# A hybrid mixer layer on one core: the rwkv chain's next state copied by ScalarE, the decayed state's share of kappa put into the next PSUM bank, and work that waits for transfers issued later

## The chip, the core and the metric

The kernel runs on one core of a Trainium2 chip. The core has TensorE (PE, matrix multiply, with its weight loads shown as PEld), VectorE (DVE), ScalarE (ACT), GpSimd (POOL) and SyncE (SP, which issues the transfers here). Each engine takes its own list of instructions in order, and semaphores hold an instruction until what it needs is done. The metric is the time of one execution on the device, in microseconds (us); lower is better.

## The reference

One layer over a sequence of 1024 frames and 1024 channels, all in float32: RMS norm, one input projection, three mixers side by side (4 heads mLSTM, 6 heads retention, 6 heads RWKV-7), output projection with residual, RMS norm, a gated feed-forward with residual, and a last RMS norm.

```python
h = rmsnorm(x, ln1_g);  p = h @ w_in
pm, pr, pw = jnp.split(p, [M_COLS, M_COLS + R_COLS], axis=-1)
y = jnp.concatenate([mlstm_group(pm, ...), retention_group(pr), rwkv7_group(pw, ...)], axis=-1)
x = x + y @ w_out
h = rmsnorm(x, ln2_g)
x = x + (jax.nn.silu(h @ w_gate) * (h @ w_up)) @ w_down
return rmsnorm(x, lnf_g)
# the recurrence inside rwkv7_group, one frame:
S = (S * w_t[:, :, None, :]
     - jnp.einsum('bhvk,bhk->bhv', S, kk_t)[..., None] * (kk_t * a_t)[:, :, None, :]
     + v_t[..., :, None] * k_t[..., None, :])
y_t = jnp.einsum('bhvk,bhk->bhv', S, r_t)
```

## The kernel before

The projections and the feed-forward split each float32 operand into a high and a low part and multiply in three matmuls (`three`, `tok_proj`, `product`); these are the bulk of PE's work. The program has two parts. In the first, up to about 767 us, the mixers run, woven into the bulk matmuls of the input and output projections. The second part is the feed-forward.

In the first part each piece of work is a Python generator. `weave` runs them against a planned clock: each `yield (cost, wait)` says how much PE time the step takes and how long until its next step is due, and names ("inv00", "yw3") are events that others wait for. The chain's wait after a chunk is `CHAIN`, after its inner steps `LAT`. Generators in `sharing` (rwkv_proj, fillers, out_proj) fill the time between. The framework's scheduler then puts each engine's instructions into one fixed list, by its own estimate of when each is ready; an instruction that waits holds up everything behind it on its engine.

RWKV works on 3 pairs of heads (i), each in two halves of 512 frames (h), each half in 8 chunks of 64 frames (c): 48 chunks in a row. For each half,

- `rwkv_half` prepares the operands: the decayed keys and queries in the big tile E, the gram matmuls between `kb` and E (L460; q is the head of the pair, and the two heads lie in the two halves of the partitions), their masks on DVE, and the transposed keys;
- `rwkv_inverse` inverts the triangular 64 x 64 blocks: the blocks go through DRAM (`ab_d`) into MN, one 32 x 32 block in each partition; ACT copies parts of MN into R (L509); 15 elimination steps on DVE work on R and MN; R goes back through DRAM (`r_d`) into E; a transpose (L535) and small matmuls (L540, L546) join the blocks;
- `rwkv_chain_pair` walks the chunks. Per chunk: kappa = E . X (L581), where X holds the state and the values of the chunk; ACT copies it to pm (L583); pm times the inverse (L586) gives the corrected values, which ACT copies into X (L592, L593); then the state's part of the output (L590), the new state (L597) and the output (L600). DVE adds the decayed old state and writes the sum into the next chunk's X (L607), POOL copies it to st (L609); ACT copies the output to yw (L610) and sums its squares (L611).

`rwkv_out` fetches the gate and the bonus and multiplies them on POOL (L638) before it waits for yw. `mlstm_load` fetches the log gates of a chunk as w, adds the causal mask on POOL (L860) and takes the exponential on ACT (L863). `norms` splits the stored output (ywt) into high and low. The rotary table `rot` is loaded once, 512 KB. PSUM has eight banks in three pools: acc (3), misc (3) and chain (2).

Of the kernel before, what the change touches and what calls it, by code (L numbers as in the profile page):

```python
# [19 lines left out]
P = 128  # L20
# [3 lines left out]
KT = 8  # L24
# [30 lines left out]
def trunk_kernel(ctx: ExitStack, tc: tile.TileContext, a: dict, out: bass.AP):  # L55
# [71 lines left out]

    def signal(name, after=0.0):
        events[name] = clock[0] + after
# [61 lines left out]
    CHAIN, INV, ATT, NORM, MIX = 3.51, 20.16, 3.09, 3.26, 1.28  # L191
# [178 lines left out]

    hv, hv_E = {}, {}
# [9 lines left out]
    def rwkv_half(i, h, r, k, v):  # L381
# [64 lines left out]
        E = big.tile([P, 8, 2, 256], F32, name="E", tag="E")  # L446
        kb = sb.tile([P, 8, 2, 64], F32, name="kb", tag="kb")
        for q in range(2):
            rows = rows_of(q)
            V.tensor_tensor(kb[rows, :, q, :], c3(th)[rows], c3(ek)[rows], ALU.mult)  # L450
            V.tensor_tensor(kb[rows, :, 1 - q, :], c3(k)[rows], c3(ek)[rows], ALU.mult)
            V.tensor_tensor(E[rows, :, q, 128:192], c3(kk)[rows], er[rows, :, 0:64], ALU.mult)
            G.tensor_tensor(E[rows, :, q, 192:256], c3(r)[rows], er[rows, :, 1:65], ALU.mult)
        yield 0.9, 5.5
        for c0 in range(0, 8, 4):
            grams = [misc_tile().rearrange("p (c x) -> p c x", c=4) for _ in two]
            for c in range(4):
                for q, g4 in enumerate(grams):
                    rows = rows_of(q)
                    PE.matmul(g4[:, c, :], lhsT=kb[rows, c0 + c, :, :].rearrange("p a t -> p (a t)"),  # L460
                              rhs=E[rows, c0 + c, q, 128:256], start=True, stop=True)
            for q, g4 in enumerate(grams):
# [3 lines left out]
                V.tensor_tensor(E[orow, cs4, q, 192:256], g4[rows, :, 0:64], msk[rows], ALU.mult)  # L466
                V.tensor_tensor(E[orow, cs4, q, 128:192], g4[orow, :, 0:64], msk[orow], ALU.mult)
                V.tensor_tensor(E[:, cs4, q, 64:128], g4[:, :, 64:128],
# [8 lines left out]
        for c0 in range(0, 8, 4):  # L477
# [4 lines left out]
            S.copy(out=E[:, c0:c0 + 4, :, 0:64], in_=pt.rearrange("p (c q d) -> p c q d", c=4, q=2))  # L482
# [7 lines left out]
    col = lambda b: slice(192 + b * 32, 224 + b * 32)  # L490
    lane = lambda g: slice(32 * g, 32 * g + 32)

    def rwkv_inverse_issue(i, h, E):
        ab_d = dram.tile([2, 2, 8, 32, 32], F32, name="ab_d", tag=f"ab_d{i}{h}")
        for q in range(2):
            for b in range(2):
                SY.dma_start(out=ab_d[b, q].rearrange("c s t -> s c t"), in_=E[blk(q, b), :, q, col(b)])
        return ab_d

    def rwkv_inverse():  # L500
        for i in range(3):
            for h in range(2):
# [5 lines left out]
                for g in range(4):  # L508
                    S.copy(out=R[lane(g)], in_=MN[lane(g), g::4, :])  # L509
# [4 lines left out]
                V.tensor_tensor(tv, mf[:, 34:34 + 15 * 66:66].unsqueeze(2).broadcast_to([P, 15, 32]), MN[:, 2:31:2], ALU.mult)  # L514
# [15 lines left out]
                for q in range(2):  # L530
                    for b in range(2):
                        SY.dma_start(out=E[blk(q, b), :, q, col(b)], in_=r_d[b, q].rearrange("c s t -> s c t"))
                yield 0.0, 7.5
                for q in range(2):
                    V.transpose(out=T11[blk(q, 0)], in_=E[blk(q, 0), :, q, col(0)])  # L535
                pqr = misc_tile()
                q3, r3 = (pqr[:, z:z + 256].rearrange("p (c t) -> p c t", c=8) for z in (0, 256))
                for c in range(8):
                    for q in range(2):
                        PE.matmul(q3[blk(q, 1), c, :], lhsT=E[blk(q, 0), c, q, col(1)], rhs=T11[blk(q, 0), c, :],  # L540
# [3 lines left out]
                for c in range(8):  # L544
                    for q in range(2):
                        PE.matmul(r3[blk(q, 0), c, :], lhsT=Q[blk(q, 1), c, :], rhs=E[blk(q, 1), c, q, col(1)],  # L546
                                  start=True, stop=True)
                for q in range(2):
                    S.copy(out=E[blk(q, 0), :, q, col(1)], in_=r3[blk(q, 0)])
# [7 lines left out]
    def rwkv_chain_pair(i):  # L557
        st = None
        for h in range(2):
# [3 lines left out]
            for c in range(8):  # L563
# [14 lines left out]
                chn = chain_tile()  # L578
                pm = sb.tile([P, 64], F32, name="pm", tag="pm", bufs=2)
                for q in range(2):  # L580
                    PE.matmul(chn[rows_of(1 - q), 0:64], lhsT=E[:, c, q, 128:192], rhs=X[:, c, q, :],  # L581
                              start=True, stop=True, skip_group_check=True)
                S.copy(out=pm, in_=chn[:, 0:64])  # L583
                yield 0.2, LAT
                for q in range(2):
                    PE.matmul(chn[rows_of(q), 64:128], lhsT=E[rows_of(1 - q), c, q, 192:256], rhs=pm[rows_of(1 - q), :],  # L586
                              start=False, stop=True, skip_group_check=True)
                for q in range(2):
                    d, o = rows_of(q), rows_of(1 - q)
                    PE.matmul(chn[o, 192:256], lhsT=E[d, c, q, 192:256], rhs=st[d, :], start=False, stop=False,  # L590
# [972 lines left out]
```

## Time and profile before

| | us |
|---|---|
| median of 3 runs (1514.54 to 1521.72) | 1515.08 |
| the profiled execution | 1521.67 |
| its span in the profile | 1519.9 |
| PE busy in it | 1425.6 |
| DVE, ACT, POOL busy | 892.4, 556.2, 437.9 |

The page of the profile gives the busy time of each engine, the chain of work that ended last, and groups of instructions by line; waits name the engine's instruction, what it waited for, the total, the times and the longest. Names such as `E<-misc` are output and input tiles of the program. The granted clock (PEclk) is the share of full speed that PE's throttle let through. Busy PE includes the modelled ends of matmuls that overlap.

### The profile page before, as it was taken

The page shows a single profiled execution, that of the slowest core. Times are in us where ns is not written, and L with a number is a line of the kernel's source. Part 1 is how long each engine was busy: PE and PEld are TensorE (multiplying, and loading weights), DVE is VectorE, ACT ScalarE, POOL GpSimd, SP SyncE. Part 2 cuts the span into 40 slices and gives each one's busy share as a digit, 9 for nine tenths or more (in the row PEclk, how much of TensorE's full clock was granted, in tenths as well). Part 3 has the DMA queues.
Part 4 walks back from the last instruction along what each step waited for, and adds up shares of the span by engine and source line. Part 5 has one row for each costly group of instructions (what it writes and reads, how often), then busy time and mean ns, then how long its engine had stood idle before and what let it go on. Part 6 is the DMA issues. An engine that isn't in the chain of part 4 may idle for free.

```text
span 1519.9 us, 23085 instructions
## 1 busy us (share of the span) xinstructions
PE 1425.6 (94%) x8434; PEld 1161.3 (76%) x8434; DVE 892.4 (59%) x1762; ACT 556.2 (37%) x1202; POOL 437.9 (29%) x539
## 2 busy tenths in 40 slices
PE   7998799789998998999998999999999998999996
PEld 5777577777777887887777887888888886887886
DVE  6457567458847756645468555555555565347434
ACT  6353334333432133244456333333333344224222
POOL 3211013234424333333545433344444420000000
PEclk9999999999978889899999999999999999999998
DMA  5142122334422244354632222222222247337333
GB/s 209 43 136 66 50 80 74 83 89 112 122 59 68 85 129 124 106 161 142 220 112 85 96 83 83 72 73 78 83 84 83 83 168 255 93 95 238 98 97 111
DMA packets 122269, 164.55 MB, mean 108 GB/s; under 512 B 38028, under 2 KB 70956, under 8 KB 120876
## 3 DMA queue, kind: packets, MB, share of 16 engines
q1 hardware_dynamic: 122156, 163.08, 33.5%
q8 instruction: 66, 1.08, 0.3%
q14 instruction: 47, 0.39, 0.1%
HBM read 124.75 MB, written 38.29 MB: 107 GB/s over the span
## 4 chain that ended last, share of the span: by engine, by line
PE 53%; DVE 3%; POOL 2%; DMA 2%; issue 1%; ACT 0%; POOLq 0%; DVEq 0%; SPq 0%; ACTq 0%
PE acc L1171 5%; PE acc L1172 5%; PE acc L1173 5%; PE chain L1365 5%; PE chain L1364 5%; PE chain L1366 5%; PE misc L1172 4%; PE misc L1171 4%; PE misc L1173 4%; PE acc L119 2%; PE acc L121 2%; PE acc L120 2%; DVE act L93 1%; PE acc L729 1%; PE acc L731 1%
## 5 line engine op out<-in xcount | busy, mean ns | idle before, releaser
L93 DVE TENSOR_TENSOR wlo<-wraw,whi 128x512 fp32r<-128x512 f32 (+1 forms) x210 | 147.9, 707 | 138.3 <-ACT whi L90 137.1
L90 ACT ACTIVATE whi<-wraw 128x512 fp32r<-128x512 f32 (+1 forms) x210 | 128.1, 612 | 226.3 <-PE chain L1365 117.9
L729 PE MATMUL acc<-whi,act 128*128 128x256 f32 (+1 forms) x512 | 161.3, 318 | 4.4 <-ACT whi L90 3.4
L90 ACT ACTIVATE whi<-rg 128x512 fp32r<-128x512 f32 x128 | 79.8, 631 | 228.7 <-POOL rg L1232 90.0
L730 PE MATMUL acc<-wlo,act 128*128 128x256 f32 (+1 forms) x512 | 155.4, 305 | 5.2 <-DVE wlo L93 5.2
L119 PE MATMUL acc<-act,whi 128*128 128x512 f32 x352 | 152.3, 433 | 7.0 <-ACT whi L90 6.2
L93 DVE TENSOR_TENSOR wlo<-rg,whi 128x512 fp32r<-128x512 f32 x128 | 93.1, 728 | 108.1 <-ACT whi L90 105.9
L731 PE MATMUL acc<-whi,act 128*128 128x256 f32 (+1 forms) x512 | 153.0, 300 | 0.0
L1364 PE MATMUL chain<-act,whi 128*128 128x512 f32 (+1 forms) x374 | 144.3, 386 | 4.0 <-ACT act L90 4.0
L120 PE MATMUL acc<-act,whi 128*128 128x512 f32 x352 | 145.5, 413 | 1.5 <-DVE act L252 1.5
L121 PE MATMUL acc<-act,wlo 128*128 128x512 f32 x352 | 145.7, 414 | 1.1 <-DVE wlo L93 1.1
L1365 PE MATMUL chain<-act,whi 128*128 128x512 f32 (+1 forms) x374 | 144.0, 385 | 0.5 <-DVE act L93 0.5
L1366 PE MATMUL chain<-act,wlo 128*128 128x512 f32 (+1 forms) x374 | 143.8, 384 | 0.0
L1171 PE MATMUL acc<-act,whi 128*128 128x512 f32 x352 | 139.3, 396 | 3.4 <-ACT pre L1432 2.7
L1173 PE MATMUL acc<-act,wlo 128*128 128x512 f32 x352 | 138.8, 394 | 0.0
L1172 PE MATMUL acc<-act,whi 128*128 128x512 f32 x352 | 138.5, 394 | 0.0
L729 PEld LDWEIGHTS acc<-whi,act 128*128 128x128 f32 x512 | 104.3, 205 | 12.1 <-ACT whi L90 3.9
L730 PEld LDWEIGHTS acc<-wlo,act 128*128 128x128 f32 x512 | 105.0, 206 | 9.2 <-DVE wlo L93 6.7
L731 PEld LDWEIGHTS acc<-whi,act 128*128 128x128 f32 x512 | 105.2, 206 | 1.0
L1172 PE MATMUL misc<-act,whi 128*128 128x512 f32 x264 | 104.1, 394 | 0.0
L1171 PE MATMUL misc<-act,whi 128*128 128x512 f32 x264 | 104.0, 394 | 0.0
L1173 PE MATMUL misc<-act,wlo 128*128 128x512 f32 x264 | 103.8, 393 | 0.0
(327 smaller groups left out, 2835.9 us busy)
## 6 DMA issues: line engine op xcount, KB each, us to landing
wraw<-in_w_down SPq DMA_DIRECT2D x85, 256.0 KB, 2.7
rg<-in_w_gate SPq DMA_DIRECT2D x22, 512.0 KB, 4.9
rg<-in_w_up SPq DMA_DIRECT2D x22, 512.0 KB, 5.0
a_dram<-work SPq DMA_DIRECT2D x41, 256.0 KB, 2.2
wraw<-in_w_tm SPq DMA_DIRECT2D x40, 256.0 KB, 3.0
rg<-a_dram SPq DMA_DIRECT2D x10, 1024.0 KB, 6.1
v_dram<-vt SPq DMA_DIRECT2D x64, 128.0 KB, 1.9
wraw<-in_w_out SPq DMA_DIRECT2D x32, 256.0 KB, 3.2
```

The lines of the kernel that those rows point to most:

```text
L90: S.activation(hi, src, AF.Copy, scale=scale)
L93: (eng or V).tensor_tensor(lo, src, hi.bitcast(F32), ALU.subtract)
L119: PE.matmul(ps, lhsT=hi, rhs=xh[:, k, :], start=(k == 0), stop=False)
L729: PE.matmul(o, lhsT=xh[h][:, k, sl], rhs=w[k][0], start=(k == 0), stop=False)
L730: PE.matmul(o, lhsT=xh[h][:, k, sl], rhs=w[k][1], start=False, stop=False)
L731: PE.matmul(o, lhsT=xl[h][:, k, sl], rhs=w[k][0], start=False, stop=(k == KT - 1))
L1171: PE.matmul(ps, lhsT=hi, rhs=hi_x[:, k, :], start=(start and k == 0), stop=False, skip_group_check=True)
L1172: PE.matmul(ps, lhsT=hi, rhs=lo_x[:, k, :], start=False, stop=False, skip_group_check=True)
L1173: PE.matmul(ps, lhsT=lo, rhs=hi_x[:, k, :], start=False, stop=(stop and k == 3), skip_group_check=True)
L1364: PE.matmul(ps, lhsT=hi, rhs=hi_a[:, sl], start=(f == 0), stop=False)
L1365: PE.matmul(ps, lhsT=hi, rhs=lo_a[:, sl], start=False, stop=False)
L1366: PE.matmul(ps, lhsT=lo, rhs=hi_a[:, sl], start=False, stop=(f == FT - 1))
```

## The change

The chunk's algebra is regrouped. X for the next chunk now holds only the new part of the state, which two ACT copies move there from the bank. The decayed old state, sd, is made on POOL at the start of the chunk; its product with the next chunk's kappa columns goes into the next chunk's bank (`nxt`) ahead, and the next chunk's kappa adds onto it (`start=first`). DVE writes only st. E is laid out so that one matmul with 128 output rows gives new state and output ("both"); the output of a head then lies beside the state of the other, and yw and Square work on half the partitions each. Beside that:

- R is loaded from `ab_d` by a transfer of its own; the four ACT copies go.
- The gram matmuls are held in the order in which the heads alternate, each issued after the one before (`tc.issue_after`).
- `late(eng)` issues what follows after the last instruction written so far on that engine. It is used for the first step of the inverse and the transposes (DVE), the product of gate and bonus (POOL), the split of ywt (ACT), and the mLSTM mask and exponential, which move out of the load into `mlstm_weights`.
- rot is loaded per frame tile, 64 KB, 24 times through two buffers.
- CHAIN is 1.4 instead of 3.51, and the planned costs of the steps are 0.4, 0.2, 0.6 instead of 0.2, 0.2, 0.4.

```diff
+    def late(eng):
+        return tc.issue_after(next(i for i in reversed(nc.cur_bb.bb.instructions) if i.engine == eng.engine))
-    CHAIN, INV, ATT, NORM, MIX = 3.51, 20.16, 3.09, 3.26, 1.28
+    CHAIN, INV, ATT, NORM, MIX = 1.4, 20.16, 3.09, 3.26, 1.28
+    kap = lambda q: slice(256 + 128 * q, 320 + 128 * q)
+    rcp = lambda q: slice(320 + 128 * q, 384 + 128 * q)
...
-                    PE.matmul(g4[:, c, :], lhsT=kb[rows, c0 + c, :, :].rearrange("p a t -> p (a t)"),
-                              rhs=E[rows, c0 + c, q, 128:256], start=True, stop=True)
+                    with tc.issue_after(prev.ins) if prev else nullcontext():
+                        prev = PE.matmul(g4[:, c, :], lhsT=kb[rows, c0 + c, :, :].rearrange("p a t -> p (a t)"),
+                                         rhs=E[rows, c0 + c, 256 + 128 * q:384 + 128 * q], start=True, stop=True)
...
-                for g in range(4):
-                    S.copy(out=R[lane(g)], in_=MN[lane(g), g::4, :])
+                SY.dma_start(out=R, in_=ab_d.rearrange("b q c (j g) t -> g (b q c) j t", g=4))
...
-                V.tensor_tensor(tv, mf[:, 34:34 + 15 * 66:66].unsqueeze(2).broadcast_to([P, 15, 32]), MN[:, 2:31:2], ALU.mult)
+                with late(V):
+                    V.tensor_tensor(tv, mf[:, 34:34 + 15 * 66:66].unsqueeze(2).broadcast_to([P, 15, 32]), MN[:, 2:31:2], ALU.mult)
...
-                chn = chain_tile()
+                chn = chain_tile() if first else nxt
+                both = lambda q: slice(128 + 64 * q, 192 + 64 * q)
...
+                if not last:
+                    nX, nE, n = (X, E, c + 1) if c < 7 else (hv[i, 1]["X"], hv[i, 1]["E"], 0)
+                    sd = sb.tile([P, 64], F32, name="sd", tag="sd", bufs=2)
+                    G.tensor_scalar(sd, st, dl[:, c:c + 1], None, ALU.mult)
...
+                if not last:
+                    nxt = chain_tile()
+                    for q in range(2):
+                        d, o = rows_of(q), rows_of(1 - q)
+                        PE.matmul(nxt[o, 0:64], lhsT=nE[d, n, kap(q)], rhs=sd[d, :], start=True, stop=False,
+                                  skip_group_check=True)
...
+                        PE.matmul(chn[:, both(q)], lhsT=E[:, c, 128 * q:128 * q + 128], rhs=X[:, c, q, :], start=False,
+                                  stop=True, skip_group_check=True)
...
-                        V.scalar_tensor_tensor(nX[d, n, q, :], in0=st[d, :], scalar=dl[d, c:c + 1],
-                                               in1=chn[d, 128:192], op0=ALU.mult, op1=ALU.add)
-                        G.tensor_copy(nst[d, :], nX[d, n, q, :])
-                S.copy(out=yw[:, c % 4, :], in_=chn[:, 192:256])
+                        S.copy(out=nX[d, n, q, :], in_=chn[d, both(q)])
+                    for q in range(2):
+                        d = rows_of(q)
+                        V.scalar_tensor_tensor(nst[d, :], in0=st[d, :], scalar=dl[d, c:c + 1], in1=chn[d, both(q)],
+                                               op0=ALU.mult, op1=ALU.add)
+                for q in range(2):
+                    o = rows_of(1 - q)
+                    S.copy(out=yw[o, c % 4, :], in_=chn[o, both(q)])
+                    S.activation(sb.tile([P, 64], F32, name="ysq", tag="ysq")[o, :], chn[o, both(q)], AF.Square,
+                                 accum_out=var[o, c % 4:c % 4 + 1])
...
+                    with late(G):
+                        G.tensor_tensor(add, add, ga, ALU.mult)
...
+            if g in (2, 3, 4):
+                rot = at.tile([P, P], F32, name="rot", tag="rot", bufs=2)
+                SY.dma_start(out=rot, in_=a["rot"][:, t, :])
...
+    def mlstm_weights(c, ws):
+        for q, w in enumerate(ws):
+            G.tensor_tensor(w, w, cc("causal").unsqueeze(1).broadcast_to([P, 2, P]), ALU.add)
+            for p in range(2):
+                hd = 2 * p + q
+                S.activation(w[:, p, :], w[:, p, :], AF.Exp, scale=-1.0, bias=mg["gs"][:, c, hd:hd + 1])
...
+                with late(S):
+                    split_hi(yh[:, 5 + i], yw)
```

The edits change every engine's list. Three places show how; line numbers of the changed kernel differ. First ACT before, in the chain of the third pair's first half, where the inverse of its second half begins:

```order
L583 COPY pm<-chain 128x64
L509 COPY R<-MN 32x256 x4
L755 ACTIVATE vt<-acc,rhalf 128x256
L592 COPY X<-chain 64x64
L593 COPY X<-chain 64x64
L90 ACTIVATE whi<-wraw 128x512 x3
```

ACT after, where the preparation of the same half ends (L491 is the copy of its transposed keys; L597 is now pm, L606 and L607 the corrected values, L631 the next X, L638 yw, L639 the squares):

```order
L491 COPY E<-misc 128x4x2x64 x2
L639 ACTIVATE ysq,yvar<-chain 64x64
L638 COPY yw<-chain 64x64
L639 ACTIVATE ysq,yvar<-chain 64x64
L597 COPY pm<-chain 128x64
L606 COPY X<-chain 64x64
L607 COPY X<-chain 64x64
L631 COPY X<-chain 64x64 x2
```

The copies of R between pm and X are gone; the next X follows the corrected values, and yw of the chunk before stands ahead of pm here.

Second PE before, one chunk of the first pair's second half (L586 to L600; L729 to L731 are bulk matmuls of a token projection):

```order
L586 MATMUL chain<-pm,E 64x64 x2
L590 MATMUL chain<-st,E 64x64 x2
L729 MATMUL acc<-whi,act 128x256 x2
L730 MATMUL acc<-wlo,act 128x256
L731 MATMUL acc<-whi,act 128x256
L597 MATMUL chain<-X,E 64x64 x2
L600 MATMUL chain<-X,E 64x64 x2
```

PE after, the end of an early chunk (L611 is the state's part of the output, L617 the decayed state's kappa for the next chunk, L625 "both"; L119 to L121 are bulk matmuls):

```order
L611 MATMUL chain<-st,E 64x64 x2
L617 MATMUL chain<-sd,E 64x64 x2
L625 MATMUL chain<-X,E 128x64 x2
L119 MATMUL acc<-act,whi 128x512
L120 MATMUL acc<-act,whi 128x512
L121 MATMUL acc<-act,wlo 128x512
```

The state's part of the output has moved from the step of pm to the last step, and new state and output are one pair of matmuls.

Third SP before, at the inverse of the second pair's first half (the names other than MN are stores and loads of the mLSTM gates and of rwkv_out):

```order
L760 DMA v_dram_90<-vt 128x256
L802 DMA mpl<-mp_d 32x1
L507 DMA MN<-ab_d 128x1x1024
L807 DMA g_d<-gl 32x128
L816 DMA d_d<-dec 32x1
L654 DMA yw_dram_83<-gate 128x256
```

SP after, at the same inverse:

```order
L507 DMA ab_d<-E 32x8x32 x4
L667 DMA gate<-gate_dram_85 128x256
L517 DMA MN<-ab_d 128x1x1024
L518 DMA R<-ab_d 128x8x32
L101 DMA wraw<-in_w_cm 128x512 x2
L683 DMA yw_dram_83<-gate 128x256
```

R is asked for right behind MN, and the mLSTM gates now come later in the program than this inverse.

More of the change, by code (lines that the diff above doesn't have):

```diff
@@ L1 @@
 import math
-from contextlib import ExitStack
+from contextlib import ExitStack, nullcontext
 from itertools import chain
@@ L481, in rwkv_half @@
                              identity=ident)
-            S.copy(out=E[:, c0:c0 + 4, :, 0:64], in_=pt.rearrange("p (c q d) -> p c q d", c=4, q=2))
+            S.copy(out=E[:, c0:c0 + 4, 0:384].rearrange("p c (q x) -> p c q x", q=2)[:, :, :, 0:64],
+                   in_=pt.rearrange("p (c q d) -> p c q d", c=4, q=2))
         hv[i, h] = dict(E=E, X=X, dl=dl)
@@ L496, in rwkv_inverse_issue @@
             for b in range(2):
-                SY.dma_start(out=ab_d[b, q].rearrange("c s t -> s c t"), in_=E[blk(q, b), :, q, col(b)])
+                SY.dma_start(out=ab_d[b, q].rearrange("c s t -> s c t"), in_=E[blk(q, b), :, col(q, b)])
         return ab_d
@@ L531, in rwkv_inverse @@
                     for b in range(2):
-                        SY.dma_start(out=E[blk(q, b), :, q, col(b)], in_=r_d[b, q].rearrange("c s t -> s c t"))
+                        SY.dma_start(out=E[blk(q, b), :, col(q, b)], in_=r_d[b, q].rearrange("c s t -> s c t"))
                 yield 0.0, 7.5
                 for q in range(2):
-                    V.transpose(out=T11[blk(q, 0)], in_=E[blk(q, 0), :, q, col(0)])
+                    with late(V):
+                        V.transpose(out=T11[blk(q, 0)], in_=E[blk(q, 0), :, col(q, 0)])
                 pqr = misc_tile()
@@ L618, in rwkv_chain_pair @@
                     yws.append(yw)
-                yield 0.4, CHAIN
+                yield 0.6, CHAIN
             signal(f"chain{i}{h}", 1.0)
@@ L768, in a_tile @@
         return at.tile([P, 384], F32, name=name, tag="a", bufs=11)[0:parts, 0:n]
-    rot = at.tile([P, KT, P], F32, name="rot", tag="rot")
-    SY.dma_start(out=rot, in_=a["rot"])
     def mlstm_gates():
@@ L1098, in attention, with weigh @@
     def attention():
+        def weigh(t, args):
+            if len(args) == 4:
+                with late(G):
+                    mlstm_weights(t, args[-1])
         mlstm = ("mlstm", 2.6, mlstm_load, mlstm_chunk, mlstm_finish, None)
@@ L1106, in attention @@
             yield 0.0, 6.0
+            weigh(ts.start, args)
+            yield 0.0, 2.0
             for t in ts:
```

62 lines of the change are left out of this document (30 added, 32 removed).

## The prediction

> **What bounds the kernel now.** I read the page first, then busy times of three stretches, then the waits of TensorE and of ScalarE in the middle stretch, where everything lies that the change touches.
>
> ```profile
> span 1519.9 us, 23085 instructions
> PE 1425.6 (94%) x8434; PEld 1161.3 (76%) x8434; DVE 892.4 (59%) x1762; ACT 556.2 (37%) x1202; POOL 437.9 (29%) x539
> core 0: us, PE busy (x) PEld busy (x) DVE busy (x) ACT busy (x) POOL busy (x), PEclk, DMA share, GB/s
> 100.00:770.00 670.00, 611.27 (x4849) 505.28 (x4849) 428.31 (x1100) 243.25 (x683) 218.26 (x361) 0.91 0.35 105
> 770.00:1520.00 750.00, 727.85 (x3200) 590.65 (x3198) 406.07 (x573) 262.62 (x435) 191.22 (x133) 0.99 0.33 109
> ```
>
> TensorE (PE) bounds the program: 94% busy. From 770 us on (feed-forward, untouched) it is 97% busy at a granted clock of 0.99. From 100 to 770 us, where the rwkv chain is woven into the projections, it idles 670 - 611.3 = 58.7 us and the clock is 0.91. The instruction lists are in fixed order, so ending the chain earlier is worth nothing by itself; only PE's idle time, its clock and its own work count. Its waits from 100 to 770 us (total, times, longest), then ScalarE's (ACT):
>
> ```profile
> PE misc L540 <- DVE tq L535: 10.5, 3, 7.7
> PE chain L597 <- ACT X L593: 7.8, 3, 6.0
> PE chain L586 <- ACT pm L583: 7.6, 5, 2.0
> PE misc L460 <- DVE E L468: 5.2, 3, 4.3
> PE chain L581 <- DVE X L607: 4.4, 1, 4.4
> PE acc L729 <- ACT whi L90: 3.4, 2, 3.0
> ACT yw L610 <- DVE X L607: 62.8, 24, 10.1
> ACT R L509 <- DMA MN<-ab_d: 27.9, 5, 8.1
> ACT w L863 <- POOL w L860: 17.2, 10, 6.0
> ```
>
> ACT serves its queue in order, so a copy that waits for a transfer holds up the chain's copies behind it. The time order of ACT around three of PE's gaps (idle time and releaser in brackets):
>
> ```profile
> 295.72 1.66 ACT L509 COPY R<-MN 32x256 f32<-32x256 f32 x4 [5.30 <-DMA MN<-ab_d]
> 372.17 0.69 ACT L863 ACTIVATE w<-w,gtok 128x128 f32<-128x128 f32 x2 [6.02 <-POOL w L860]
> 373.90 0.19 ACT L583 COPY pm<-chain 128x64 f32<-128x64 f32 x1
> 488.89 1.66 ACT L509 COPY R<-MN 32x256 f32<-32x256 f32 x4 [5.13 <-DMA MN<-ab_d]
> 594.03 1.65 ACT L509 COPY R<-MN 32x256 f32<-32x256 f32 x4 [6.80 <-DMA MN<-ab_d]
> 596.08 0.19 ACT L592 COPY X<-chain 64x64 f32<-64x64 f32 x1
> ```
>
> The 6.0 us wait of PE L597 ends at 596.6, after X at 596.08, which stood behind the R copies; pm at 373.90 stood behind the exponentials L863.
>
> **The change part by part.**
>
> *R by a transfer, and the mLSTM weights issued late.* No ACT instruction of the chain then stands behind a transfer of MN or of w. What can go: the waits of PE on pm (7.6), on X (7.8) and the 3.0 us on whi that ended with the R copies at 488.89. That is 18.4 us, bounds -18.4 and 0; I take all of it, because each of these gaps ends in the ACT rows behind L509 or L863. The price is R's own landing. The nearest transfer is the way back of the same tile in pieces of the same size:
>
> ```profile
> 634.70 4.89 DMA r_d<-R
> ```
>
> 4.89 us against 1.65 us of copies, and the first two VectorE (DVE) steps need MN alone, so the inverse may come up to 3 us later, six times; its reader L540 already waited 10.5 us in three of six. Bounds -2 (R lands with MN, the copies' time is won) to +18; I take +2, nearer to the low end, since R's 128 KB are asked for right behind MN's 512 KB and should land close to them.
>
> *Kappa no longer reads what DVE wrote.* Today kappa (L581) waits for L607 on DVE; the one wait of 4.4 us stood behind a scan held by a transfer:
>
> ```profile
> 279.65 0.16 DVE L798 TENSOR_TENSOR_SCAN mp<-m 4x8 f32<-4x8 f32 x1 [5.50 <-DMA m<-bl_d]
> 281.08 0.29 DVE L607 SCALAR_TENSOR_TENSOR X<-st,dl,chain 64x64 f32<-64x64 f32 x1
> ```
>
> After the change two ACT copies take its place. -4.4; bounds -4.4 and +4.4 (the same stall met one step later, through yw, below).
>
> *ACT gets more work.* Per chunk two copies for the next X are added and yw, Square and the accumulator read come twice:
>
> ```profile
> L592 ACT COPY X<-chain x48: 188/205/211, 170.6 to 730.8; 64x64 f32<-64x64 f32 x48
> L610 ACT COPY yw<-chain x48: 192/212/232, 172.4 to 735.5; 128x64 f32<-128x64 f32 x48
> L611 ACT ACTIVATE ysq<-chain x48: 205/230/257, 172.5 to 735.6; 128x64 f32<-128x64 f32 x48
> L611 ACT ACTIVATION_READ_ACCUMULATOR ysq<-chain x48: 193/204/224, 172.6 to 735.7; 128x1 f32 x48
> ```
>
> 2 x 0.21 + 0.21 + 0.23 + 0.20 = 1.06 us, times 45 to 48 is about 50 us, less 10 us for the six R copies: ACT goes from 243 to about 283 of 670 us, 42%. I cost it at nothing: 58% of ACT's time there is idle and covers it; without that cover it is up to 1 us a chunk.
>
> *TensorE's own work.* Per chunk L597 and L600 (four rows each) go; two matmuls "both" of 128 output rows and two of the decayed state come:
>
> ```profile
> 193.53 0.34 PE L597 MATMUL chain<-X,E 128*64 128x64 f32 x4
> 193.69 0.29 PE L600 MATMUL chain<-X,E 128*64 128x64 f32 x4
> 193.91 0.50 PE L119 MATMUL acc<-act,whi 128*128 128x512 f32 x1
> 198.25 0.34 PE L581 MATMUL chain<-X,E 128*64 128x64 f32 x4
> 268.68 1.16 PE L460 MATMUL misc<-E,kb 64*128 64x128 f32 x16
> 271.64 1.16 PE L460 MATMUL misc<-E,kb 64*128 64x128 f32 x8
> ```
>
> From 193.53 to 193.91 the eight old ones take 0.38 us. By L581 the two new groups take between 0.3 and 0.55 us: +0.1 a chunk, x45 = +4.5, bounds -4 and +8. The gram matmuls (L460) gain: 16 that alternate between the two row halves took 1.16 us, 8 of one half alone also 1.16. About seven blocks now run one half after the other (in the order after, only the first matmul of a block stands alone): 7 x 0.9 = -6, bounds -7.6 and 0 (0 if a joint block waits for both banks).
>
> *The clock.* After many a gap the granted clock is halved (columns as in the stretches above; the last but two is the clock):
>
> ```profile
> 279.70:286.50 6.80, 5.07 (x24) 4.73 (x26) 2.93 (x7) 2.07 (x7) 3.21 (x4) 0.50 0.14 34
> 491.30:501.50 10.20, 10.02 (x53) 8.58 (x54) 6.45 (x19) 3.06 (x12) 3.60 (x5) 0.50 0.37 122
> 593.70:600.50 6.80, 3.94 (x23) 3.83 (x24) 5.29 (x15) 4.93 (x14) 1.52 (x4) 0.50 0.18 60
> 600.50:607.30 6.80, 6.80 (x65) 6.01 (x63) 5.68 (x19) 3.19 (x9) 2.06 (x3) 1.00 0.44 141
> L730 PE MATMUL acc<-wlo,act 128*128 128x256 f32 x4 | 1.7, 415 | 0.0
> L730 PE MATMUL acc<-wlo,act 128*128 128x256 f32 x8 | 2.3, 293 | 0.0
> ```
>
> The last two rows are L730 in these two stretches: 415 against 293 ns, so a halved microsecond loses 0.29. A clock of 0.91 over 670 us is 670 x 0.09 / 0.5 = 120 us halved, 35 us lost. Five halved stretches follow the gaps that go, the first at 279.7, the last at 593.7, 34 us together: 10 us; I take half, -5, bounds 0 and -10, as the rest of the 120 us has other causes that can strike there too. [...]
>
> *rot by pieces, the rest issued late.* 24 loads of 64 KB instead of one of 512 KB, each behind the DVE reads of two tiles before in SP's queue, in which the stores of vt already wait for later work of the same tile. Zero, bounds 0 and +5. The gate product on GpSimd (POOL) and split_hi of ywt stand behind transfers less: zero, bounds -3 and 0.
>
> *The new order.* The planner's CHAIN goes from 3.51 to 1.4, so chunks stand closer. Waits that the present order doesn't have will arise: I take +7, between 0 and the 58.7 - 18.4 - 4.4 = 36 us of other idle time, nearest to the single DVE stall of 4.4 us and one more like it.
>
> **Sum:** -18.4 + 2 - 4.4 + 4.5 - 6 - 5 + 7 = -20.3 us. The profiled execution took 1521.67 us (1.8 around its span), 6.6 above the median of 1515.08; the difference goes against either: 1501.4 on the profile's, 1494.8 on the median's. I predict 1495.
>
> **Rivals.**
>
> *The idle time is only dealt anew (no change).* For it: 36 us of idle time have other causes, L540 and L460 among them, whose transfers stay; a tighter chain puts PE's waits on them elsewhere. Against it: the 18.4 us have one named cause each. It needs +27 instead of +7 from the new order: about 1515.
>
> *The chain still hangs on DVE, through yw (slower).* The row of ACT's waits shows it: yw waits 62.8 us, 24 times, for L607, though it doesn't read what L607 writes; both read one PSUM bank. After the change nst on DVE reads the bank between the X copies and yw, and where yw stands ahead of the next pm on ACT, a late DVE makes pm late and PE waits at the next step. Today 4.3 us of matmuls (193.91 to 198.25) lie between a chunk's end and the next kappa; the new order leaves about 6 to 12 matmuls of 0.23 us. If 24 waits of 2.6 us become PE's, less 1.4 us each that six matmuls cover, that is +29; uncovered +63. In place of the +7 the sum is then -27.3 + 29 to 63: 1517 to 1551, middle 1534. It is slower from 35 us on, 0.8 us a chunk. Against it: the delays of DVE are mostly under a microsecond, and the order after puts many yw behind the next pm. [...]
>
> *More comes back than I count.* Gaps at the inverse shrink and the clock stays up: all favourable bounds give -18.4 - 2 - 4.4 - 4 - 7.6 - 10 = -46: 1469.
>
> **How the numbers follow.** A measurement here tells 0.5% (7.6 us) from no change: faster is below 1507.5, slower above 1522.7. Likeliest (1470 to 1507): 0.66. Still faster: 0.03. Dealt anew: 0.17. Hung on DVE: 0.14. So faster 0.69, same 0.17, slower 0.14. The range 1470 to 1523 leaves out the fastest case and most of the slow one; the likeliest one's own range is 1478 to 1507.
>
> **What would show it.** PE's waits on pm and X from 100 us to the end of the mixer sum below 5 us (18.4 step right); no ACT wait on MN or on w's POOL add of several us; the clock of that stretch above 0.92; gram blocks of 16 in about 1.2 us; L540's waits not above 15 us. The forecast is wrong if PE waits for pm behind yw, if waits on R or E transfers grow, or if PE's idle time from 100 us stays near 59 us.

## The result, and the profile after

The changed kernel takes 1543.5 us (median of four runs, 1532.94 to 1548.36) against 1516.09 of the kernel before in the same session: ratio 1.0154, interval 1.0119 to 1.0189. It is slower, where 1495 was forecast. A second session with six runs (told below) gave 1538.43 and 1.0158 (1.0118 to 1.0198). One of the twelve runs of the version with state and output apart (below) took 1966.5 us at a mean clock of 0.633; the figures given for it are those of the other eleven.

The profiled execution took 1532.94 us, the fastest of the four, while the profiled one of before was the slowest of its runs. So the two traces show 11 us of difference where the medians show 27; the sum at the end comes back to this. The head of the page and the middle stretch (100 to 770 us) of the changed kernel:

```profile
span 1531.2 us, 23312 instructions
PE 1436.9 (94%) x8434; PEld 1166.7 (76%) x8434; DVE 888.4 (58%) x1762; ACT 594.5 (39%) x1412; POOL 428.8 (28%) x494
100.00:770.00 670.00, 613.59 (x4816) 504.25 (x4815) 417.63 (x1092) 274.19 (x880) 200.61 (x310) 0.93 0.36 107
```

The bound is what it was: PE busy 94%. The first matmul of the feed-forward marks the end of the part that the change touches. Here are both kernels' (before first, then after):

```profile
811.45 0.39 PE L1171 MATMUL acc<-act,whi 128*128 128x512 f32 x1
823.97 0.39 PE L1214 MATMUL acc<-act,whi 128*128 128x512 f32 x1
```

It comes 12.5 us later, and from there to the end the two spans have 708.5 and 707.2 us. The whole loss lies ahead of it. Busy times from 100 us to that matmul, before and after (columns as in the stretches above):

```profile
100.00:811.50 711.50, 652.77 (x5030) 539.09 (x5030) 457.70 (x1138) 266.21 (x721) 234.56 (x371) 0.92 0.35 106
100.00:824.00 724.00, 663.22 (x5027) 544.64 (x5026) 455.08 (x1138) 303.59 (x929) 224.54 (x326) 0.93 0.36 107
```

PE's idle time is 711.5 - 652.8 = 58.7 us before and 724.0 - 663.2 = 60.8 after; its work grew by 10.5 us. A second trace of the changed kernel, from the second session, has 722.9 - 667.8 = 55.1 us of idle time: two traces of one kernel differ by 5.7 us, so a smaller difference of idle time between two kernels, one trace each, shows nothing. The main waits of PE after, 100 to 770 us (total, times, longest), and three of ACT's:

```profile
PE misc L551 <- DVE tq L546: 9.3, 2, 6.4
PE acc L762 <- DVE wlo L93: 7.7, 4, 5.4
PE misc L919 <- DVE w L911: 5.2, 3, 3.1
PE chain L611 <- ACT X L607: 4.9, 1, 4.9
PE misc L402 <- ACT t L399: 4.8, 4, 3.4
PE acc L761 <- ACT whi L90: 4.2, 2, 2.8
PE misc L908 <- DMA mq<-mqk_dram: 3.2, 1, 3.2
PE chain L604 <- ACT pm L597: 1.7, 3, 0.9
ACT X L606 <- PE chain L604: 51.2, 31, 4.5
ACT yw L638 <- DVE st L634: 26.9, 23, 3.5
ACT w L897 <- POOL w L894: 14.5, 9, 6.1
```

The waits on pm and X fell from 15.4 to 6.6 us, as the first step said, and others took their place: mq is new, and those on wlo, w and t grew (before 5.2, 1.1 and 2.0 us). PE waits less for the chain, yet it stands still about as long as before. ACT's wait for DVE ahead of yw fell from 62.8 to 26.9 us, and PE waited for pm only 1.7 us: in this trace the chain does not hang on DVE.

Where PE's work grew is read from the groups of the chain's matmuls by line and shape (busy us and mean ns of one; before first):

```profile
L581 PE MATMUL chain<-X,E 128*64 128x64 f32 x192 | 17.8, 255 | 4.4 <-DVE X L607 4.4
L586 PE MATMUL chain<-pm,E 64*64 64x64 f32 x192 | 16.9, 247 | 7.7 <-ACT pm L583 7.6
L597 PE MATMUL chain<-X,E 128*64 128x64 f32 x180 | 16.0, 260 | 7.8 <-ACT X L593 7.8
L600 PE MATMUL chain<-X,E 128*64 128x64 f32 x192 | 15.6, 238 | 0.0
L590 PE MATMUL chain<-st,E 64*64 64x64 f32 x192 | 15.0, 224 | 0.5 <-POOL st L609 0.5
L625 PE MATMUL chain<-X,E 128*128 128x64 f32 x180 | 30.5, 294 | 0.0
L611 PE MATMUL chain<-st,E 64*64 64x64 f32 x192 | 18.0, 246 | 5.0 <-ACT X L607 4.9 <-DVE st L634 0.2
L604 PE MATMUL chain<-pm,E 64*64 64x64 f32 x192 | 17.7, 252 | 1.8 <-ACT pm L597 1.7
L595 PE MATMUL chain<-X,E 128*64 128x64 f32 x192 | 17.6, 255 | 0.4 <-ACT X L631 0.3
L617 PE MATMUL chain<-sd,E 64*64 64x64 f32 x180 | 14.0, 226 | 1.6 <-ACT w L897 0.8 <-POOL sd L601 0.6
```

The five lines of before sum to 81.3 us; after, with 1.2 us of the last chunks' output (L622), to 99.0. In time order one chunk's third group reads, after:

```profile
201.58 0.40 PE L121 MATMUL acc<-act,wlo 128*128 128x512 f32 x1
201.91 0.33 PE L611 MATMUL chain<-st,E 64*64 64x64 f32 x4
202.07 0.28 PE L617 MATMUL chain<-sd,E 64*64 64x64 f32 x4
202.28 0.66 PE L625 MATMUL chain<-X,E 128*128 128x64 f32 x4
202.75 0.48 PE L119 MATMUL acc<-act,whi 128*128 128x512 f32 x1
```

From 201.91 to 202.75 it takes 0.84 us, against 0.38 us of the two rows quoted of before (193.53 to 193.91); it also holds st's rows, which before stood beside pm's. The two matmuls "both" (four rows a chunk, 180 in 45 chunks) alone take 202.28 to 202.75. The trace lists them as 128*128, 128 rows and 128 columns of the array, and the rows of before (L597, L600) as 128*64. That the two heads therefore no longer run side by side is my reading of the gram rows of the prediction, of which 16 that alternate between the halves took 1.16 us, as long as 8 of one half. The rows of the weight loads (PEld) are longer too, 0.52 us for the four of "both" against 0.20:

```profile
201.91 0.20 PEld L611 LDWEIGHTS chain<-st,E 64*64 64x64 f32 x4 [0.37 <-ACT cv L724]
202.28 0.52 PEld L625 LDWEIGHTS chain<-X,E 128*128 128x128 f32 x4
```

A price list comes from all chunks that lie between two bulk matmuls at full clock without a gap (19 to 31 of each kind; start of the group to start of the next bulk matmul, medians): before, kappa 0.264, pm with st 0.378, state with output 0.380, in all 1.02 us; after, kappa 0.265, pm 0.262, st with sd and both 0.846, in all 1.37 us. Four more rows of 64 output rows in a group cost 0.118 us, the four of "both" 0.468; the last row ahead of another shape costs 0.148 to 0.152 instead of 0.052. The price is four times as high and not twice, so a lost place beside the other head would not be all of it. The longer weight loads may be a part, by my estimate; no run separates them. So the chain's work rose by 0.35 us a chunk, 15.8 us in 45 chunks, where I had taken 4.5.

### The profile page after: what moved, and what is told of

It is laid out like the page before. It is cut to its first block, busy times and chain, and to the rows that moved or that the text cites. A ratio compares the mean times of both kernels' runs of the same rounds, so it can differ in the third digit from the quotient of the medians.

```text
span 1531.2 us, 23312 instructions
## 1 busy us (share of the span) xinstructions
PE 1436.9 (94%) x8434; PEld 1166.7 (76%) x8434; DVE 888.4 (58%) x1762; ACT 594.5 (39%) x1412; POOL 428.8 (28%) x494
## 4 chain that ended last, share of the span: by engine, by line
PE 62%; DMA 6%; DVE 5%; issue 4%; POOL 4%; ACT 1%; SPq 1%; POOLq 0%; DVEq 0%; ACTq 0%
PE acc L1214 5%; PE acc L1215 5%; PE acc L1216 5%; PE chain L1408 5%; PE chain L1407 5%; PE chain L1409 5%; PE misc L1215 4%; PE misc L1214 4%; PE misc L1216 4%; PE acc L119 3%; PE acc L121 2%; PE acc L120 2%; PE acc L762 2%; PE acc L761 2%; PE acc L763 2%
## 5 line engine op out<-in xcount | busy, mean ns | idle before, releaser
L761 PE MATMUL acc<-whi,act 128*128 128x256 f32 (+1 forms) x512 | 156.9, 308 | 6.4 <-ACT whi L90 4.2
L762 PE MATMUL acc<-wlo,act 128*128 128x256 f32 (+1 forms) x512 | 152.3, 299 | 7.8 <-DVE wlo L93 7.7
L119 PE MATMUL acc<-act,whi 128*128 128x512 f32 x352 | 152.3, 433 | 5.8 <-ACT whi L90 5.8
L763 PE MATMUL acc<-whi,act 128*128 128x256 f32 (+1 forms) x512 | 150.0, 295 | 0.0
L121 PE MATMUL acc<-act,wlo 128*128 128x512 f32 x352 | 144.3, 410 | 1.1 <-DVE wlo L93 1.1
L761 PEld LDWEIGHTS acc<-whi,act 128*128 128x128 f32 x512 | 100.7, 197 | 13.5 <-ACT whi L90 4.7
L762 PEld LDWEIGHTS acc<-wlo,act 128*128 128x128 f32 x512 | 101.4, 198 | 10.9 <-DVE wlo L93 8.7
L763 PEld LDWEIGHTS acc<-whi,act 128*128 128x128 f32 x512 | 101.3, 199 | 1.3 <-issue 0.2
```

The lines of the kernel that those rows point to most:

```text
L119: PE.matmul(ps, lhsT=hi, rhs=xh[:, k, :], start=(k == 0), stop=False)
L761: PE.matmul(o, lhsT=xh[h][:, k, sl], rhs=w[k][0], start=(k == 0), stop=False)
L762: PE.matmul(o, lhsT=xh[h][:, k, sl], rhs=w[k][1], start=False, stop=False)
L763: PE.matmul(o, lhsT=xl[h][:, k, sl], rhs=w[k][0], start=False, stop=(k == KT - 1))
```

## The experiments

Theory A: the regrouped chain loses by its own work on PE (A1: by the 128 rows of "both"; A2: by the number of groups and by sd), while idle time is only dealt anew. Rivals: B, the side edits (R's transfer, rot, late issue) lose; C, the denser plan loses; D, that every order meets other late transfers, so that named waits can't be added up; E, that the clock is lower as such (D and E are named in later runs only). Ratios are to the kernel before in the same session (1514.6 to 1515.8 us).

**All edits but the chain.** The kernel before, with every hunk of the diff but those of E's layout, `rwkv_chain_pair` and the plan's numbers:

```diff
+                    with tc.issue_after(prev.ins) if prev else nullcontext():
...
+                SY.dma_start(out=R, in_=ab_d.rearrange("b q c (j g) t -> g (b q c) j t", g=4))
...
+                with late(V):
...
     CHAIN, INV, ATT, NORM, MIX = 3.51, 20.16, 3.09, 3.26, 1.28
```

> The kernel before with every edit but the regrouped chain: R by a transfer, joint gram matmuls, late issue, mLSTM weights late, rot by pieces; the chain's own algebra and CHAIN 3.51 as before. Theory A (the regrouped chain puts some 19.5 us of extra work on TensorE, while its idle time is only dealt anew): this kernel keeps the gram gain of 6.5 us and loses nothing, so 1500 to 1510, ratio 0.990 to 0.997, chain work in TensorE near 55 us. Theory B (the loss is in the side edits: R's landing, rot's 24 loads, late issue): 1525 to 1545 here as well. Theory C (the loss is in the denser plan, CHAIN 1.4): 1500 to 1510 here too, so run 3 tells it from A.

1514.92 us, ratio 1.000 (0.9976 to 1.0024). B falls. But the gain of the grams, for which A gave 1500 to 1510, is not there either.

**The chain alone**, with its plan and rot by pieces (the diff is against the changed kernel, as in all runs that start from it).

```diff
-                    with tc.issue_after(prev.ins) if prev else nullcontext():
...
-                SY.dma_start(out=R, in_=ab_d.rearrange("b q c (j g) t -> g (b q c) j t", g=4))
+                for g in range(4):
+                    S.copy(out=R[lane(g)], in_=MN[lane(g), g::4, :])
...
-                with late(V):
...
```

> The changed kernel with only the regrouped chain, its plan (CHAIN 1.4) and rot by pieces (for room); R by copies, grams free in order, no late issue, weights in the load. Theory A: TensorE's chain work is 74 us as in the changed kernel and the grams cost 6.5 us more: 1540 to 1555, ratio 1.017 to 1.026. Theory B: 1510 to 1520. Theory C: the same as A, told apart by run 3.

1536.41 us, ratio 1.0148 (1.0113 to 1.0184): nearly all of the loss, though less than the 1540 to 1555 of A.

**The plan of before.**

```diff
-    CHAIN, INV, ATT, NORM, MIX = 1.4, 20.16, 3.09, 3.26, 1.28
+    CHAIN, INV, ATT, NORM, MIX = 3.51, 20.16, 3.09, 3.26, 1.28
...
-                yield 0.4, LAT
+                yield 0.2, LAT
...
-                yield 0.6, CHAIN
+                yield 0.4, CHAIN
```

> The changed kernel with the plan of before: CHAIN 3.51 and planned costs of 0.2, 0.2, 0.4 instead of 1.4 and 0.4, 0.2, 0.6. Theory A: the instructions are the same, TensorE's chain work stays within 3 us of 74, and the time stays within 8 us of the changed kernel (1535 to 1550). Theory C: the time falls to 1510 to 1522, since the waits for tq, wlo, t and w that came with the new order go.

1535.55 us, ratio 1.014 (1.0106 to 1.0174). C falls: the loss stays with the chain.

**st's matmuls beside pm's again.**

```diff
-                S.copy(out=X[0:64, c, 0, :], in_=chn[0:64, 64:128])
-                S.copy(out=X[64:128, c, 1, :], in_=chn[64:128, 64:128])
-                yield 0.2, LAT
                 for q in range(2):
                     d, o = rows_of(q), rows_of(1 - q)
                     PE.matmul(chn[o, both(q)], lhsT=E[d, c, rcp(q)], rhs=st[d, :], start=False, stop=False,
                               skip_group_check=True)
+                S.copy(out=X[0:64, c, 0, :], in_=chn[0:64, 64:128])
+                S.copy(out=X[64:128, c, 1, :], in_=chn[64:128, 64:128])
+                yield 0.2, LAT
```

> The changed kernel with one edit: the state's two matmuls (st) are written behind pm's again, as in the kernel before, instead of beside sd's and both's. Theory A, and that rows of pm and st in opposite halves run side by side: pm falls from 0.147 to about 0.09 us a chunk and st's 0.12 stay, so 45 x 0.06 = 2.7 us and up to 5.7 us less TensorE work, 3 to 8 us faster than the changed kernel. Rival (pm costs more because of what stands ahead of it, not what stands behind): no change in TensorE's chain work, 74 us.

1538.22 us, ratio 1.0158 (1.0114 to 1.0201): no gain, where A gave 3 to 8 us. By the price list a chunk's groups take as long as before: pm with st 0.378 and sd with both 0.730, against pm 0.262 and st, sd and both 0.846, which is 1.11 us either way. There are two groups in both orders, and moving st's rows from one to the other gave nothing here.

**State and output apart.**

```diff
-                        PE.matmul(chn[:, both(q)], lhsT=E[:, c, 128 * q:128 * q + 128], rhs=X[:, c, q, :], start=False,
-                                  stop=True, skip_group_check=True)
+                        PE.matmul(chn[rows_of(q), both(q)], lhsT=E[:, c, 192 * q:192 * q + 64], rhs=X[:, c, q, :],
+                                  start=False, stop=True, skip_group_check=True)
+                if not last:
+                  for q in range(2):
+                    o = rows_of(1 - q)
+                    PE.matmul(chn[o, both(q)], lhsT=E[:, c, 64 + 64 * q:128 + 64 * q], rhs=X[:, c, q, :], start=False,
+                              stop=True, skip_group_check=True)
```

> The changed kernel with one edit: the two matmuls of 128 output rows (both) become four of 64 rows, state and output apart, over the same columns of E. Theory A1 (in undisturbed chunks the 128-row pair takes 0.468 us, while 64-row pairs that alternate between the halves of the array add 0.118 us a pair): 0.468 - 0.236 = 0.23 us less a chunk, x45 = 10.4 us: 1526 to 1531 if the changed kernel stands at 1538, ratio to the kernel before 1.007 to 1.012; chain work in TensorE 64 us instead of 74. Rival A2 (the cost is the number of groups and the extra sd products, not the rows): within 3 us of the changed kernel, 1535 to 1543.

1522.86 us, ratio 1.004 (1.0017 to 1.0063): 15 to 17 us of the 23 go, with one edit. It is faster than the 1526 to 1531 of A1. Its third group in time order:

```profile
200.08 0.33 PE L611 MATMUL chain<-st,E 64*64 64x64 f32 x4
200.24 0.28 PE L617 MATMUL chain<-sd,E 64*64 64x64 f32 x4
200.46 0.34 PE L625 MATMUL chain<-X,E 128*64 128x64 f32 x4
200.62 0.29 PE L630 MATMUL chain<-X,E 128*64 128x64 f32 x4
200.84 0.50 PE L119 MATMUL acc<-act,whi 128*128 128x512 f32 x1
```

200.08 to 200.84 is 0.76 us, only 0.08 below the changed kernel's 0.84: the change of shape from 64*64 to 128*64 costs its price again (0.22 us from L617 to L625, against 0.16 from L611 to L617, which have one shape). That is 3.9 us in 45 chunks, not the 10.4 that I expected. By work alone the other 11.9 of the 15.8 us stay, with the added group and sd (A2); less the 6 us that the grams save, that is the 6 us that this version still loses. But the time falls by more than the 3.9 us; by its halved time (below) the clock would account for some 8 us of the rest.

**The price by itself.** The kernel before with rows that nobody reads, of 64 and of 128 output rows:

```diff
+                for q in range(2):
+                    PE.matmul(chn[rows_of(1 - q), 256:320], lhsT=E[:, c, q, 64:128], rhs=X[:, c, q, :], start=False,
+                              stop=True, skip_group_check=True)
```

> The kernel before with two matmuls of 64 output rows added per chunk behind L600, into unused columns of the chain's bank; nobody reads them, so no wait is added. Theory A: every TensorE microsecond there is on the path, 48 x 0.118 = 5.7 us: 1520 to 1522. Rival (TensorE's idle time of 59 us takes it up): 1515, no change.

```diff
+                for q in range(2):
+                    PE.matmul(chn[:, 256 + 64 * q:320 + 64 * q], lhsT=E[:, c, q, 0:128], rhs=X[:, c, q, :], start=False,
+                              stop=True, skip_group_check=True)
```

> As the run above, but the two added matmuls have 128 output rows (columns 0 to 127 of E for each head). Theory A1: 48 x 0.468 = 22.5 us: 1535 to 1540. Rival A2 (128 rows cost what 64 rows cost): 1520 to 1522. Rival (idle time takes it up): 1515.

1517.77 us, ratio 1.0023 (1.000 to 1.0047), and 1532.59 us, 1.0105 (1.0077 to 1.0132). In time 0 to 7 us for the 64-row pair (5.7 expected) and 12 to 20 for the 128-row one (22.5 expected). In the traces a pair adds 0.12 and 0.47 us to its group, as in the price list; in all, the added rows (L603) are 14.5 and 34.9 us busy. For twice the output rows the work is four times as long, and the time added clearly longer; that is A1's point without the regrouped chain. The rival that idle time takes the work up is out for the 128-row pair, and open for the 64-row one.

**The grams alone.**

```diff
+                    with tc.issue_after(prev.ins) if prev else nullcontext():
+                        prev = PE.matmul(
...
```

> The kernel before with the joint gram matmuls alone. If the gain of 5 to 6 us of TensorE work is kept: 1508 to 1510, ratio 0.995 to 0.997. If the holding in order costs waits of its own, or the idle time is dealt anew as in the first run: 1515, ratio 1.000.

1518.05 us, ratio 1.0023 (0.9996 to 1.0049): no gain, although the work is saved. The gram group of before, and of this run:

```profile
L460 PE MATMUL misc<-E,kb 64*128 64x128 f32 x192 | 23.3, 312 | 7.5 <-DVE E L468 5.2 <-DVE E L452 2.2
L462 PE MATMUL misc<-E,kb 64*128 64x128 f32 x192 | 18.2, 310 | 4.6 <-DVE E L452 2.2 <-DVE R L524 1.6 <-DVE E L470 0.7
```

There are 5.1 us less work, and PE's idle time to the feed-forward is 63.1 us instead of 58.7; a wait on pm of 7.5 us is new. That idle time took up the gain fits, but with one trace each it is not shown.

**Without sd.** State and output apart, and:

```diff
-                    G.tensor_scalar(sd, st, dl[:, c:c + 1], None, ALU.mult)
...
-                        PE.matmul(nxt[o, 0:64], lhsT=nE[d, n, kap(q)], rhs=sd[d, :], start=True, stop=False,
-                                  skip_group_check=True)
```

> The run with state and output apart (both split), and beside that the decayed state's part left out: no sd on POOL and no product of it with the next kappa, so that kappa lacks the decayed old state (that part of the computation is missing). The copies on ScalarE, the new order and CHAIN 1.4 stay. Theory A: sd's pairs cost 0.118 us a chunk, 45 x 0.118 = 5.3 us of the 7.6 us by which the split kernel stands above the kernel before: 1515 to 1520, ratio 1.000 to 1.003. Rival (ScalarE's 50 us of added work or the tighter plan costs the rest): 1522 to 1526, as with sd.

1517.32 us, ratio 1.0017 (1.0001 to 1.0033). From 1.004 the ratio falls by some 3.5 us, where 5.3 was expected; the two intervals overlap, so sd's price is likely, not settled. ACT still does all its added copies here; together with all else that is left of the change, gains included, they cost at most 5 us.

**The two edits on which my largest term stood.** R's transfer and the late weights, on the kernel before:

```diff
+                SY.dma_start(out=R, in_=ab_d.rearrange("b q c (j g) t -> g (b q c) j t", g=4))
...
+            weigh(ts.start, args)
+            yield 0.0, 2.0
...
```

> The kernel before with two edits alone: R by a transfer and the mLSTM mask and exponential issued late. My sum gave them -18.4 + 2 us of TensorE waits: 1499. Theory D (TensorE's idle time is dealt anew: another copy that waits for a transfer, such as decr behind dfull, is met at the same place): the waits on pm and X fall by less than half or others grow by as much, TensorE's idle time from 100 us to the feed-forward is 54 to 63 us as in all runs so far, and the time is 1511 to 1519.

1511.69 us, ratio 0.9975 (0.9953 to 0.9998): 4 us gained, not 16. PE still waits 13.6 us for pm and X (15.4 before); its longest wait, from 303.0 to 311.5 us, is again on X. The copies of decr, which wait for the transfer of dfull, now stand ahead of X on ACT:

```profile
PE chain L600 <- ACT X L596: 8.9, 3, 8.5
310.25 0.42 ACT L825 COPY decr<-dfull 64x16 f32<-64x16 f32 x2 [10.52 <-DMA dfull<-d_d]
```

**One more late copy.** All edits but the chain, and the copies of decr moved:

```diff
-            S.copy(out=decr[rows_of(q)], in_=dv[rows_of(q), q])
...
+        if c == 0:
+            for q in range(2):
+                S.copy(out=mg["decr"][rows_of(q)], in_=mg["dv"][rows_of(q), q])
```

> The first run (all edits but the chain) with one more: the two copies of decr on ScalarE, which waited 5.33 us for dfull at 300.8 us and made TensorE wait 4.85 us for X at 296.9, are written with the first mLSTM weights instead. If that wait is time on the path: 4.85 us less, 1508 to 1511. Theory D: something else is late, idle time stays in 54 to 63 us, 1512 to 1518.

1516.33 us, ratio 0.9999 (0.9973 to 1.0025). The stall near 300 us shows best what happens. First ACT in the kernel before, then in the first run (all edits but the chain), then ACT and PE in this run, then ACT in the changed kernel:

```profile
300.44 0.40 ACT L822 COPY decr<-dfull 64x16 f32<-64x16 f32 x2
300.80 0.42 ACT L830 COPY decr<-dfull 64x16 f32<-64x16 f32 x2 [5.33 <-DMA dfull<-d_d]
301.24 0.21 ACT L599 COPY X<-chain 64x64 f32<-64x64 f32 x1
305.51 0.42 ACT L872 COPY decr<-dfull 64x16 f32<-64x16 f32 x2 [5.66 <-DMA dfull<-d_d]
306.63 0.58 PE L740 MATMUL acc<-whi,act 128*128 128x256 f32 x1 [3.73 <-ACT whi L90]
300.49 0.47 ACT L787 ACTIVATE vt<-acc,rhalf 128x256 f32<-128x256 f32 x1 [5.28 <-DMA mqk_dram<-mth]
300.86 0.19 ACT L606 COPY X<-chain 64x64 f32<-64x64 f32 x1
```

In the kernel before, decr stood behind the copies of R, which waited 5.30 us for MN, and behind an exponential, which waited 1.79 us for w; it did not wait itself. Where those are gone it waits 5.33 us for dfull and holds up X. In this run it is only moved: it still waits 5.66 us, until 305.51, and holds up whi, for which PE waits 3.7 us. In the changed kernel vt waits 5.28 us for another transfer there. Taking one reader out of the queue put the next in front. Since this run's copies still wait for dfull, it does not tell what the kernel would take without that wait.

**Another order of the same instructions.** The kernel before with one number changed:

```diff
-    CHAIN, INV, ATT, NORM, MIX = 3.51, 20.16, 3.09, 3.26, 1.28
+    CHAIN, INV, ATT, NORM, MIX = 3.0, 20.16, 3.09, 3.26, 1.28
```

> The kernel before with one number changed: CHAIN 3.0 instead of 3.51, so the same instructions stand in another order. It measures what a new order alone deals. Theory D: idle time 54 to 63 us, time 1510 to 1522 (ratio within 0.5% of 1). Rival (a tighter plan costs idle time, or gains it, in proportion): 1505 or below, or 1525 or above.

1507.61 us, ratio 0.9959 (0.9937 to 0.9981): a gain of 6 us from a number, a little below D's 1510 to 1522, with 51.8 us of idle time. The changed kernel again:

> The changed kernel as it is, once more. Its four runs stood at 1533 to 1548 with mean clocks of 0.958 to 0.945; over all kernels so far a run's time rises by some 0.35 to 0.4 us for each us in which the clock is halved. Theory E (128-row pairs hold the clock down): halved time near 150 us against 130 of the kernel before, time 1538 to 1546. If the four runs were chance: halved time 130, as in the 12 undisturbed runs of the split kernel, and 1532 to 1537.

1538.43 us, 1.0158 (1.0118 to 1.0198); halved time 147.5 us on the mean of six runs. The lower clock was not chance: E holds for this order. With the plan's numbers of the changed kernel (CHAIN 1.4; 0.4, 0.2, 0.6) on the kernel before:

> The kernel before with the changed kernel's plan alone: CHAIN 1.4 and planned costs of 0.4, 0.2, 0.6. My sum gave the new order +7, with bounds 0 and +36: 1522. Theory D (an order deals idle time anew within some 10 us either way): 1505 to 1525. If a tighter plan is good by itself, as CHAIN 3.0 was (1507.6): 1500 to 1508.

1519.75 us, 1.002 (0.9992 to 1.0048). With CHAIN 2.5:

> The kernel before with CHAIN 2.5, between the two. A trend with the number would give a time between those of CHAIN 3.0 and of 1.4; a deal gives any time from 1505 to 1525.

1503.23 us, 0.9924 (0.9903 to 0.9946): the fastest version, below both kernels and just below the 1505 to 1525 of a deal; a trend with the number is out. With CHAIN 3.0, R's transfer and the late weights:

> The kernel before with R by a transfer, the mLSTM weights late (1511.7 alone) and CHAIN 3.0 (1507.6 alone). If the two gains are of named waits and add up: 1504 to 1506. If both are deals of the order: anything from 1505 to 1518, idle time 50 to 63 us.

1518.44 us, 1.001 (0.9981 to 1.0039): two gains of 6 and 4 us, together none. So CHAIN 3.51, 3.0 and 2.5 give 1515, 1508 and 1503, and 1.4 with its step costs 1520. Over the 16 runs, before and after, PE's idle time to the feed-forward stays between 51.8 and 63.1 us. Named gains do not add up, as D says; its ranges were narrowly missed three times (1507.6, 1503.2, 1518.4). How much of the spread of idle time is the order and how much the single execution is open, since two traces of one kernel differ by 5.7 us. The shortest time has longer waits on pm than the kernel before (11.4 against 7.6 us):

```profile
PE chain L586 <- ACT pm L583: 11.4, 3, 6.9
PE misc L540 <- DVE tq L535: 7.7, 1, 7.7
core 0: 1505.3 us, clock 0.962
```

**The clock over all runs.** Each run has a span and a mean clock. In the traces of before and after the clock is 1.0 or 0.5 throughout; taken so for every run, 2 x (1 - clock) x span is the time for which it was halved. Its mean is 128.9 us for the kernel before (35 runs), 152 and 147.5 for the changed one (4 and 6 runs), 130.3 with state and output apart (11), 100.6 with CHAIN 2.5 (12, standard error 1.9). Among the runs of one kernel the time rises by 0.25 to 0.46 us for each halved microsecond (eleven kernels of 11 or 12 runs; the kernel before 0.33 to 0.37 over 17 to 35). At 0.4 the changed kernel loses some 8 us by its clock, its split version none, and CHAIN 2.5 wins 11 us, all that it wins. But CHAIN 3.0 gained 6 us at 130.9, and the plan with 1.4 stood 3 us above the kernel before at 121: the clock is not all that an order changes. What in the order or in the 128-row pairs sets the clock is open: the run with added 128-row pairs stood at 133 (6 runs), that with the chain alone at 135, those with the plan of before and with st beside pm at 149 and 151.

## Why the prediction was wrong, step by step

The step that failed first is "TensorE's own work", +4.5 with bounds -4 and +8. It measured 15.8 us at full clock. I priced the two new groups together by one row of L581, as 64-row pairs that share the array. By the price list the 0.35 us a chunk are three things. One more group has its own start and end, since st's rows left pm's and "both" has another shape than sd: 0.14 us, or 6.5 in 45 chunks. sd's own rows cost 0.12 us, or 5.3. "Both" stands against state and output with 0.47 to 0.38 us, which is 3.9. In the row that I quoted of before, four and four matmuls took 0.38 us, where four alone take 0.26: the second four cost 0.12. Its eight rows share one start and one end (the 0.14 us above), which the regrouping gave up; that its two heads run side by side is my reading, which no run shows by itself. The upper bound was too low for the same reason. In time "both" weighs more than its 3.9 us, for 15 to 17 us went with it when it was taken apart; the lower clock, some 8 us, is a part of that, and its cause is open.

The second is "R by a transfer, and the mLSTM weights issued late", -18.4. Half of its signs came: PE waits for pm and X 6.6 us instead of 15.4, most of it one wait of 4.9. But the exponentials, issued late, still hold ACT behind POOL for 14.5 us, up to 6.1 at a time (before 17.2 and 6.0). The time did not follow: the two edits alone gained 4 us, and idle time, 58.7 us before, is 60.8 and 55.1 in the two traces after. I had argued that each gap "ends in the ACT rows behind L509 or L863". That was so, but I did not look at what stood next in ACT's queue: near 300 us it was decr, which needs dfull, and with the two edits alone PE waited 8.5 us behind it. The rival "dealt anew" described this half; I gave it 0.17.

"The clock", -5: halved time in the two profiles does fall (mean clock of the stretch 0.91 and 0.93), but the profiles are the extremes of their runs. Over the runs it rose by some 20 us, +8 us of time. My 0.29 us for a halved microsecond lies below most of the 0.25 to 0.46 of the runs.

"The gram matmuls", -6: the work fell as said (23.3 to 16.7 us in the trace's busy time), and alone it brought no time at all. "Kappa no longer reads what DVE wrote", -4.4: the wait fell to 0.4 us, in the same deal. R's landing, +2: L551's waits total 9.3 us, before 10.5. ACT's added work, zero: 274 of 670 us, forecast 283; without sd the kernel stands at 1.0017 with all these copies. rot and late issue, zero: the first run. "The new order", +7: the plan with CHAIN 1.4 on the kernel before gave +3 (-1 to +7), so +7 is at the end of its interval; with bounds of 0 and +36 I held a gain for impossible, and CHAIN 2.5 gained 11.

The rival "hung on DVE through yw" named 1517 to 1551, and the result lies there, but its mechanism did not occur: its mark, PE waiting for pm, is 1.7 us. A right number of a wrong cause. What I held against it, that DVE's delays are mostly under a microsecond, was misread: 62.8 us in 24 waits are 2.6 us each.

The sum as measured: +15.8 for the chain's work, -6 for the grams, +2 or -4 of idle time by the two traces, +8 of clock: +14 to +20, against +24 (18 to 30) by the second session. Some 4 to 10 us are not accounted for. Against the forecast, the chain's work came out 11 us higher, idle time (-13.8 forecast) 10 to 16 us, and the clock (-5) 13 us.

## What to carry to other kernels

On an engine that bounds, price a regrouped matmul from rows of its own shape (here 0.468 us for the four 128-row ones of "both", against 0.118 for four added rows of 64) and by the groups and changes of shape that it adds (0.148 to 0.152 us for the last row ahead of another shape, against 0.052), not by the number of matmuls that it saves. In a woven program don't sum waits as gains: ask which transfer ends at that moment and what stands next in the queue, and try several orders of the same instructions before any edit, since one number of the plan, CHAIN from 3.51 to 2.5, moved the kernel before by 12 us.

## What the hardware showed

A halved clock doesn't need an idle gap that the profile shows. In the traces of before and after, each of the ten longest gaps of PE between 100 and 800 us (five of each trace, 3.5 to 7.7 us) comes with a halved stretch that starts within it or less than 2 us behind it, and all stretches there last 3.4 us or a multiple, up to 17.1. But there are also stretches of 10.2 us with no gap over 0.8 us ahead of them and PE busy throughout, as this one of the changed kernel, at a clock of 0.50:

```profile
398.00:408.00 10.00, 10.00 (x78) 7.54 (x78) 2.31 (x4) 3.79 (x12) 0.69 (x1) 0.50 0.14 48
```

The largest gap in the 8 us ahead of it is 0.8 us. Busy time counts the modelled ends of matmuls, so PE can be emptier than it looks; what sets such a stretch off is not shown by these runs.
